# One trunk layer in fp32 on one core: where the newest pooling columns, the last channel sums and the first squares stand in their queues

## The chip, the core and the metric

The kernel runs on one core of a Trainium2 chip. The core has a matrix engine (TensorE; PE in the profile, its weight loads PEld), a vector engine (VectorE, DVE), an engine for functions and copies (ScalarE, ACT), a general engine (GpSimd, POOL) and a queue that mostly issues transfers (SyncE, SP). Each engine works through its own instructions in the order in which they were written into its queue; between engines they wait for each other by semaphores. The time of a run is the device time in microseconds (us) of one execution; less is better.

## The reference

One layer of a decoder trunk, for 256 columns of a new sequence and 8 x 4 newest tokens of running ones, together T = 288 columns:

```python
h = rmsnorm(x, norm1_g)
proj = h @ w_in + b_in                    # 2048 -> 3072
a, gate, z = proj[:1024], proj[1024:2048], proj[2048:]
u = a * sigmoid(gate)
c = silu(layernorm(depthwise_causal_conv(u_ext, conv_w, conv_b), ln_g, ln_b))   # 31 taps
d = multiscale_pool(z_ext)                # window means (2, 4, 8, 16) less z, 4 groups of 256 channels
p = (d @ pool_w, by group) * pool_scale
x = x + concat(c, p) @ w_out              # 2048 -> 2048
f = square(relu(rmsnorm(x, norm2_g) @ w_ff1))     # 2048 -> 8192
x = x + f @ w_ff2                         # 8192 -> 2048
y = rmsnorm(x, norm_f)
```

The last 30 columns of u and the last 15 of z are outputs as well. Everything is fp32.

## The kernel before

Channels lie on the 128 partitions, the 288 columns along the free axis. Each product of fp32 numbers is made of three products of rounded ones: a number is split into a high part (a rounded copy) and a low part (what is left), and TensorE adds up high x high, low x high and high x low. So each weight tile of 128 x 1024 numbers (a *part*, four blocks of 128 rows by 256 output channels) is loaded by SyncE, cast to its high part by ScalarE (L274, in `split_part`), and its low part is made in one of three *ways*: V, one subtraction on VectorE (L279); G, two subtractions of half a part on GpSimd (L282); D, a negated copy on ScalarE (L276) onto which GpSimd's queue adds the weights with an accumulating transfer (L277). `WAYS` (line 73) gives the way of each part by stage, in letters that repeat: stage "p" (the pooling groups without an entry of their own) has "GVVG". There are five buffers for split parts (line 101, `wspl`), and they are filled in the order in which TensorE uses them. The split of the next stage's weights is written down at the end of the present stage's `gemm`.

The input projection runs in the order of `SEQUENCE`: c0 c1 c2 c3 c4 p3 c5 p2 P3 c6 p1 P2 p0 P1 c7 P0. A *c* stage multiplies the columns of `a` and `gate` for 128 conv channels; a lower-case *p* stage the two blocks of z of one pooling group; a capital *P* is the small product of that group's differences with `pool_w`. A p or c stage is 16 blocks of rows by two banks by three products, four parts in all; each part is used over a quarter of the stage. The list `chain` sets TensorE's order to the order of writing up to P1. All else is ordered by a planner, which sorts instructions on each engine by a priority (the place in the program, moved by `later(...)`) and its own costs; `tc.issue_after(x)` puts an instruction behind x in the queue of x's engine.

`pool_group(g)` has these steps: the gemm; `tz`, bank times row factor, on VectorE (L483); z = tz + bias on ScalarE (L486, L487); the window sums by doubling, one add for each half and each doubling, on GpSimd (L492; group 1, window 4, has 4 adds, group 2 has 6, group 3 has 8); the first columns rescaled on GpSimd (L496); the difference for the sequence's columns on VectorE (L497); two steps on GpSimd for the newest columns (L499 scales, L500 subtracts), which overlap the same tile and stand behind L497; then the high copy (L502) and low part (L503).

`conv_pair(i)` scales its two banks by the row factor (L445), makes the gate's sigmoid (L447) and u (L449), and then, at a priority 1,000,000 later, 31 multiply-adds on VectorE for the sequence (L461) and one multiply on GpSimd (L464) with a reduction on VectorE (L466) for the newest columns. `sum_c` collects the channel sums for the layernorm's mean on GpSimd (L469 for pairs, L472 for the last ones).

At the start nine matmuls on constants (L214) run while inputs arrive. `first_split` casts and splits the first weights and the input; `squares` and `rsqrt_sums` make the first row factors from ScalarE's squares, TensorE's sums and a square root with a Newton step (L233 to L236 or the like); `spread` copies the factors to all partitions by three matmuls. In the layernorm `ln_mean`, `ln_sums` and `ln_rows` run between blocks of w_out's first gemms (`BETWEEN`), which start with the pooled half. At the end the last row sums give the factors of the final norm, and `finish` multiplies and stores the output in pieces.

Of the kernel before, what the change touches and what calls it, by code (L numbers as in the profile page):

```python
# [9 lines left out]
F32 = mybir.dt.float32  # L10
# [62 lines left out]
WAYS = {"c2": "GVGV", "c3": "GDGG", "c4": "GDGD", "p3": "GDDG", "c5": "GDGD", "c": "GGGV", "p": "GVVG", "w0": "VV", "w": "GG", "ff": "VV"}  # L73
# [13 lines left out]
def trunk_kernel(ctx: ExitStack, tc: tile.TileContext, io):  # L87
# [119 lines left out]
    def load_table(func, src):  # L207

        return nc.scalar.activation(few[: src.shape[0], :], src, func)

    load_table(AF.Sqrt, ones[:, 0:1])
    warm = ms("warm")
    for j in range(9):
        nc.tensor.matmul(warm[:, 0, 0:P], ones, ones, start=True, stop=True)  # L214
# [16 lines left out]
    def inverse_root(mean, root, y, out):  # L231

        nc.vector.reciprocal(y, root)  # L233
        nc.vector.scalar_tensor_tensor(out=root, in0=mean, scalar=EPS, in1=y, op0=ALU.add, op1=ALU.mult)
        nc.vector.scalar_tensor_tensor(out=root, in0=root, scalar=-0.5, in1=y, op0=ALU.mult, op1=ALU.mult)
        nc.vector.scalar_tensor_tensor(out=out, in0=root, scalar=1.5, in1=y, op0=ALU.add, op1=ALU.mult)  # L236

    def rsqrt_sums(parts, scale, after=None):

        pq = ms("pt")
        pt = pq[:, 0, :]
        for n, t in enumerate(parts):
            for j in range(3):
                last = mm(pt[:TB, j : j + 1], t[:, j * TB : (j + 1) * TB], ones[:, 0:1], start=n + j == 0, stop=n == len(parts) - 1 and j == 2)
        st = const.tile([TB, 12], F32, name=nm("st"))
        s = [st[:, 3 * j : 3 * j + 3] for j in range(4)]
        nc.vector.tensor_scalar(s[0], pt[:TB, 0:3], scale * DC, EPS, op0=ALU.mult, op1=ALU.add)
        nc.scalar.activation(s[1], s[0], AF.Sqrt)  # L250
        if after is not None:
            load_table(after, s[1][:, 0:1])
        nc.vector.reciprocal(s[2], s[1])
        nc.vector.tensor_tensor(s[3], s[2], s[2], op=ALU.mult)
        nc.vector.scalar_tensor_tensor(out=s[3], in0=s[3], scalar=-0.5, in1=s[0], op0=ALU.mult, op1=ALU.mult)
        nc.vector.scalar_tensor_tensor(out=s[2], in0=s[3], scalar=1.5, in1=s[2], op0=ALU.add, op1=ALU.mult)
        return s[2], pq[:, 1, :T], last
# [8 lines left out]
    turns = {}  # L266

    def split_part(raw, src, hi, lo, way):
# [6 lines left out]
        if way == "D":  # L275
            nc.scalar.activation(lo, f32(hi), AF.Copy, scale=-1.0)  # L276
            nc.gpsimd.dma_start(lo, src, accum_op=ALU.add)  # L277
        elif way == "V":
            nc.vector.tensor_tensor(lo, raw, f32(hi), op=ALU.subtract)  # L279
        else:  # L280
            for j in range(0, raw.shape[1], 2):
                nc.gpsimd.tensor_tensor(lo[:, j : j + 2, :], raw[:, j : j + 2, :], f32(hi[:, j : j + 2, :]), op=ALU.subtract)  # L282
# [74 lines left out]
    hx, firsts = [], []  # L357

    def first_split(k0):
# [5 lines left out]
        for k in range(k0, k0 + 2):  # L365
            if k == 0:
                nc.vector.tensor_scalar(hx[k][0], xT[:, k, :], v("norm1_g", k), None, op0=ALU.mult)  # L367
            else:
                nc.scalar.activation(hx[k][0], xT[:, k, :], AF.Copy, scale=v("norm1_g", k))  # L369
        for b in blocks[1:]:  # L370
            nc.scalar.copy(hi[:, b], raw[:, b])
        for b in blocks:
            nc.vector.tensor_tensor(lo[:, b], raw[:, b], f32(hi[:, b]), op=ALU.subtract)
# [37 lines left out]
    def squares():  # L411

        nc.scalar.copy(scratch[:, :, :, 0:1], f32(firsts[2][0])[:, 1, 1, 0:10].rearrange("p (n k t) -> p n k t", n=5, t=1))
        for q in range(8):
# [3 lines left out]
            nc.scalar.activation(dst, xq, AF.Square)  # L418
# [21 lines left out]
    def conv_pair(i, banks):  # L440
        up = u_all[:, i, 0:UO]
        us = samples(u_all[:, i, UO:UL], US)
        ta, gate = [b[:, :T] for b in banks]
        for b in (gate, ta):
            nc.vector.tensor_tensor(b, b, rb, op=ALU.mult)  # L445
        tg = tmpp.tile([P, 2, T], F32, name=nm("tg"), tag="ag", bufs=2)[:, 0, :]
        nc.scalar.activation(tg, gate, AF.Sigmoid, bias=v("b_in", 8 + i))  # L447
        for out, a, b in ((up[:, CH:UO], ta[:, :SEQ], tg[:, :SEQ]), (us[:, :, CH:US], samples(ta[:, SEQ:T], NS), samples(tg[:, SEQ:T], NS))):
            nc.vector.scalar_tensor_tensor(out=out, in0=a, scalar=v("b_in", i), in1=b, op0=ALU.add, op1=ALU.mult)  # L449
# [3 lines left out]
        with later():  # L453
# [10 lines left out]
            nc.gpsimd.tensor_tensor(prd[:, :, :, 0:CW], windows(us, CW), cwv[:, None, None, :].to_broadcast([P, NB, NS, CW]), op=ALU.mult)  # L464
# [12 lines left out]
    def pool_group(g):  # L477
# [17 lines left out]
        first_sums = s[:, :, PH : PH + w - 1]  # L495
        nc.gpsimd.tensor_tensor(first_sums, first_sums, rcnt[:, None, w - 2 : 2 * w - 3].to_broadcast([P, 2, w - 1]), op=ALU.mult)  # L496
        nc.vector.scalar_tensor_tensor(out=d[:, :, 0:SEQ], in0=s[:, :, PH:ZO], scalar=1.0 / w, in1=z[:, :, PH:ZO], op0=ALU.mult, op1=ALU.subtract)  # L497
        news = [x[:, :, ZO:ZL].rearrange("p m (b t) -> p m b t", t=ZS)[:, :, :, PH:] for x in (s, z)]
        nc.gpsimd.tensor_scalar(news[0], news[0], 1.0 / w, None, op0=ALU.mult)  # L499
        nc.gpsimd.tensor_tensor(d[:, :, SEQ:T].rearrange("p m (b t) -> p m b t", t=NS), news[0], news[1], op=ALU.subtract)  # L500
        dh, dl = act2("dx", tag="p", bufs=4)
        nc.scalar.copy(dh, d)  # L502
        nc.vector.tensor_tensor(dl, d, f32(dh), op=ALU.subtract)  # L503
        dd[g] = dh, dl

# [18 lines left out]
    def first_sums():  # L524
        diag.append(rsqrt_sums(squares(), 1.0 / D, AF.Sigmoid))
# [22 lines left out]
    load_table(AF.Sqrt, f32(mixp[1][0])[:, 0:1])  # L548
# [12 lines left out]
    def ln_sums():  # L561
        ssc = None
        for c in cs:
            nc.vector.tensor_tensor(c, c, norm["mean"][:, None, :].to_broadcast([P, 2, T]), op=ALU.subtract)
            q = tmpp.tile([P, 2, T], F32, name=nm("q2"), tag="ag" if ssc is None else "ag2", bufs=2)
            nc.scalar.activation(q, c, AF.Square)
            if ssc is None:
                ssc = q
            else:
                nc.vector.tensor_tensor(ssc, ssc, q, op=ALU.add)  # L570
        nc.vector.tensor_tensor(ssc[:, 0, :], ssc[:, 0, :], ssc[:, 1, :], op=ALU.add)
        norm["sums"] = rsqrt_sums([ssc[:, 0, :]], 1.0 / DC, AF.Silu)
        return norm["sums"][2]

    def ln_rows():
        norm["rows"], last = spread(norm["sums"])
        return last

    BETWEEN = {5: {4: ln_mean}, 6: {6: ln_sums}, 7: {2: ln_rows}}
# [10 lines left out]
    for j, c in enumerate(cs):  # L590
        n = tmpp.tile([P, 2, T], F32, name=nm("n"), tag="ag", bufs=2)
        nc.vector.tensor_tensor(n, c, norm["rows"][:, None, :].to_broadcast([P, 2, T]), op=ALU.mult)  # L592
        for m in range(2):
            i = 2 * j + m
            nc.scalar.activation(n[:, m, :], n[:, m, :], AF.Silu, bias=v("ln_b", i), scale=v("ln_g", i))  # L595
        mh, ml = act2("mx")
        nc.scalar.copy(mh, n)  # L597
# [40 lines left out]
    def second_rows():  # L638
# [9 lines left out]
        nc.scalar.activation(root, mean, AF.Sqrt, bias=eps)  # L648
        inverse_root(mean, root, r2, r2)
# [134 lines left out]
```

## Time and profile before

| what | value |
|---|---|
| median of 3 runs | 1084.99 us (1084.27 to 1086.06) |
| profiled execution | 1084.57 us, span 1082.8 us |
| TensorE busy | 1071.5 us in 8198 matmuls |
| VectorE, ScalarE, GpSimd busy | 635.4, 479.0, 173.6 us |
| HBM read, written | 185.16 MB, 4.28 MB |

The span is the time from the first to the last recorded instruction. Rows of a timeline begin with the start in us from the span's start and the duration; then come engine, line, operation, "out<-in" by the program's names, sizes, the count of merged instructions, and in brackets the idle time before and what ended it. A row of the waits says who waited for whom, how long in all, how often. The pooling stages and the conv lie in the first 200 us; w_out, w_ff1 and w_ff2 fill the rest.

### The profile page before, as it was taken

Reading aid. Unit: us, or ns where it says so; the run is one execution under the profiler, and the core shown is the slowest. Engines: PE = TensorE matmul, PEld = TensorE weight load, DVE = VectorE, ACT = ScalarE, POOL = GpSimd, SP = SyncE. Lnnn points to the kernel's source line nnn. Section 1 sums busy time; section 2 is a strip of 40 time slices with the busy share of each in tenths; the row PEclk is TensorE's granted clock in tenths of the full one; section 3 lists DMA queues with packets and bytes.
Section 4 is the critical chain, followed back from the end, with each engine's and each line's share of the span. In section 5 each row is a group of like instructions: output and inputs, shape, how many; then the busy total and the mean of one; then the engine's idle time right before and its main releaser. Section 6 shows DMA issues by size and latency. Waiting matters only on the chain.

```text
span 1082.8 us, 19572 instructions
## 1 busy us (share of the span) xinstructions
PE 1071.5 (99%) x8198; PEld 1069.9 (99%) x8198; DVE 635.4 (59%) x818; ACT 479.0 (44%) x585; POOL 173.6 (16%) x180
## 2 busy tenths in 40 slices
PE   9999999999999999999999999999999999999996
PEld 9999999999999999999999999999999999999996
DVE  8899999678655544445544444545544445554553
ACT  8654445475544433334443333444433334444441
POOL 0878979512000000000000000000000000000001
PEclk9999999999999999999999999999999999999998
DMA  9896468545555555555555555555555555555522
GB/s 325 281 273 185 137 196 239 176 152 177 173 164 170 172 166 169 174 164 169 171 168 168 175 165 169 174 167 167 174 165 168 174 169 165 173 166 168 173 78 88
DMA packets 58296, 190.71 MB, mean 176 GB/s; under 512 B 6240, under 2 KB 11232, under 8 KB 58208
## 3 DMA queue, kind: packets, MB, share of 16 engines
q1 hardware_dynamic: 56336, 184.35, 53.9%
q0 software_dynamic: 1008, 3.67, 1.9%
q8 instruction: 64, 1.05, 0.4%
q10 hardware_dynamic: 864, 1.44, 0.4%
q14 instruction: 24, 0.20, 0.1%
HBM read 185.16 MB, written 4.28 MB: 175 GB/s over the span
## 4 chain that ended last, share of the span: by engine, by line
PE 77%; issue 20%; ACT 1%; DVE 0%; DMA 0%; POOL 0%; POOLq 0%
PE ac L305 77%; PE pp L305 1%; DMA wr<-in_w 0%; ACT whi L274 0%; POOL xT L720 0%; ACT n L595 0%; DVE wlo L279 0%; PE pt L305 0%; PE pmean L305 0%; POOLq L770 0%; DVE xT L695 0%; DVE n L592 0%; ACT whi L364 0%; ACT mx L597 0%; DVE hx L367 0%
## 5 line engine op out<-in xcount | busy, mean ns | idle before, releaser
L274 ACT CAST whi<-wr 128x1024 fp32r<-128x1024 f32 (+1 forms) x332 | 348.0, 1049 | 551.4 <-PE ac L305 533.5
L279 DVE TENSOR_TENSOR wlo<-wr,whi 128x1024 fp32r<-128x1024 f32 x288 | 353.1, 1226 | 348.5 <-ACT whi L274 348.5
L305 PE MATMUL ac<-ax,whi 128*128 128x288 f32 x2048 | 351.0, 292 | 0.0
L305 PE MATMUL ac<-fx,whi 128*128 128x288 f32 x2048 | 350.2, 292 | 0.0
L305 PEld LDWEIGHTS ac<-ax,whi 128*128 128x128 f32 x2048 | 296.0, 187 | 0.0
L305 PEld LDWEIGHTS ac<-fx,whi 128*128 128x128 f32 x2048 | 295.6, 187 | 0.0
L305 PE MATMUL ac<-ax,wlo 128*128 128x288 f32 x1024 | 217.4, 292 | 0.0
L305 PE MATMUL ac<-fx,wlo 128*128 128x288 f32 x1024 | 216.4, 292 | 0.0
L305 PEld LDWEIGHTS ac<-ax,wlo 128*128 128x128 f32 x1024 | 162.6, 187 | 0.0
L305 PEld LDWEIGHTS ac<-fx,wlo 128*128 128x128 f32 x1024 | 162.3, 187 | 0.0
L305 PE MATMUL ac<-hx,whi 128*128 128x288 f32 x768 | 131.8, 295 | 1.2 <-DVE hx L367 1.2
L720 POOL TENSOR_TENSOR xT<-xT,rf 128x288 f32<-128x288 f32 x4 | 3.1, 795 | 800.1 <-ACT rf L724 800.1
L305 PEld LDWEIGHTS ac<-hx,whi 128*128 128x128 f32 x768 | 112.1, 190 | 1.4 <-ACT hx L369 1.4
L282 POOL TENSOR_TENSOR wlo<-wr,whi 128x512 fp32r<-128x512 f32 x74 | 100.3, 1410 | 35.3 <-ACT whi L274 34.3
L461 DVE SCALAR_TENSOR_TENSOR pc<-u_all,vec,pc 128x256 f32<-128x256 f32 x232 | 99.5, 483 | 1.9 <-ACT pc L458 0.7
L305 PE MATMUL ac<-hx,wlo 128*128 128x288 f32 x384 | 80.1, 294 | 0.0
L305 PEld LDWEIGHTS ac<-hx,wlo 128*128 128x128 f32 x384 | 61.1, 190 | 0.0
L305 PE MATMUL ac<-dx,whi 128*128 128x288 f32 x256 | 46.0, 296 | 0.0
L305 PE MATMUL ac<-mx,whi 128*128 128x288 f32 x256 | 45.1, 294 | 0.1
L664 DVE SCALAR_TENSOR_TENSOR t<-ac,r 128x576 f32<-128x576 f32 x32 | 24.2, 758 | 25.1 <-PE ac L305 25.1
L305 PEld LDWEIGHTS ac<-dx,whi 128*128 128x128 f32 x256 | 38.0, 188 | 0.2
L305 PEld LDWEIGHTS ac<-mx,whi 128*128 128x128 f32 x256 | 37.5, 188 | 0.6 <-ACT mx L597 0.4
(133 smaller groups left out, 533.6 us busy)
## 6 DMA issues: line engine op xcount, KB each, us to landing
wr<-in_w SPq DMA_DIRECT2D x335, 512.0 KB, 3.8
wlo<-in_w POOLq DMA_DIRECT2D x7, 512.0 KB, 7.7
xT<-in_xT SPq DMA_DIRECT2D x8, 288.0 KB, 7.3
wr<-in_w SPq DMA_DIRECT2D x5, 256.0 KB, 3.6
out_u_out<-u_all SPq DMA_DIRECT2D x1, 1208.0 KB, 9.3
u_all<-in_hist_c SPq DMA_DIRECT2D x8, 136.0 KB, 6.2
out_z_out<-z_all SPq DMA_DIRECT2D x1, 668.0 KB, 9.9
z_all<-in_hist_p SPq DMA_DIRECT2D x4, 152.0 KB, 7.5
```

Of the source, the lines that this page charges most:

```text
L274: nc.scalar.copy(hi, raw)
L279: nc.vector.tensor_tensor(lo, raw, f32(hi), op=ALU.subtract)
L282: nc.gpsimd.tensor_tensor(lo[:, j : j + 2, :], raw[:, j : j + 2, :], f32(hi[:, j : j + 2, :]), op=ALU.subtract)
L305: last = nc.tensor.matmul(*args, **kw)
L461: nc.vector.scalar_tensor_tensor(out=dst, in0=up[:, w : w + SEQ], scalar=cwv[:, w : w + 1], in1=pc, op0=ALU.mult, op1=ALU.add)
L664: nc.vector.scalar_tensor_tensor(out=t, in0=bk[:, :, :T], scalar=0.0, in1=both(rows2[0]), op0=ALU.max, op1=ALU.mult)
L720: eng.tensor_tensor(xk, xk, r[:, None, :].to_broadcast([P, n, T]), op=ALU.mult)
```

## The change

- `pool_group`: GpSimd's two steps on the newest columns (L499, L500) are written ahead of VectorE's difference (L497), so that the difference now stands behind them; for groups 1 and 0 all steps from L496 on have a priority 1,000,000 earlier. The difference is kept in `behind_pool`, and each low part of way V that is written afterwards is put behind it in VectorE's queue.
- `WAYS`: c2's fourth part becomes L, a subtraction on VectorE that is written later, behind the first bank scalings; c3's and c4's second parts go from D to V; c7 and p0 get their own entries, "GGGG" and "GVGG".
- `conv_pair`: the last two channel sums are written with the last channel block and put behind its multiply on GpSimd. The bank scalings of the first four banks move to `first_rows`.
- Start: 13 warm-up matmuls instead of 9; each square stands behind a high part of the input on ScalarE, the first low parts behind the first high part on VectorE.
- `inverse_root`: the reciprocal square root comes from one function of ScalarE, with the same Newton step; the reciprocal on VectorE is gone. All four norms use it, and the constants' placement changes with it.
- Layernorm: `ln_rows` two blocks earlier; the silus of the second to fourth pair stand behind the previous pair's copy on ScalarE.
- End: one output piece of two blocks is cut in two.

```diff
-WAYS = {"c2": "GVGV", "c3": "GDGG", "c4": "GDGD", "p3": "GDDG", "c5": "GDGD", "c": "GGGV", "p": "GVVG", "w0": "VV", "w": "GG", "ff": "VV"}
+WAYS = {"c2": "GVGL", "c3": "GVGG", "c4": "GVGD", "p3": "GDDG", "c5": "GDGD", "c7": "GGGG", "c": "GGGV", "p0": "GVGG", "p": "GVVG", "w0": "VV", "w": "GG", "ff": "VV"}
...
-    load_table(AF.Sqrt, ones[:, 0:1])
+    load_table(AF.Abs_reciprocal_sqrt, ones[:, 0:1])
     warm = ms("warm")
-    for j in range(9):
+    for j in range(13):
...
-    def inverse_root(mean, root, y, out):
-        nc.vector.reciprocal(y, root)
...
+    def inverse_root(mean, y, t, out, after=None):
+        nc.scalar.activation(y, mean, AF.Abs_reciprocal_sqrt, bias=eps[: y.shape[0], :])
+        if after is not None:
+            load_table(after, y[:, 0:1])
+        nc.vector.scalar_tensor_tensor(out=t, in0=mean, scalar=EPS, in1=y, op0=ALU.add, op1=ALU.mult)
...
         elif way == "V":
-            nc.vector.tensor_tensor(lo, raw, f32(hi), op=ALU.subtract)
+            with tc.issue_after(behind_pool[0]) if behind_pool else nullcontext():
+                nc.vector.tensor_tensor(lo, raw, f32(hi), op=ALU.subtract)
+        elif way == "L":
+            late.append((lo, raw, f32(hi)))
...
+            with tc.issue_after(scaled_x[min(q + 2, 7)]):
+                nc.scalar.activation(dst, xq, AF.Square)
...
-            if i == N8 - 2:
-                for part in (sum_c[:, 1, :], c):
-                    nc.gpsimd.tensor_tensor(sum_c[:, 0, :], sum_c[:, 0, :], part, op=ALU.add)
+            if i == N8 - 1:
+                for part in (sum_c[:, 1, :], cs[i // 2][:, 0, :]):
+                    with tc.issue_after(multiplied.ins):
+                        nc.gpsimd.tensor_tensor(sum_c[:, 0, :], sum_c[:, 0, :], part, op=ALU.add)
...
-        nc.vector.scalar_tensor_tensor(out=d[:, :, 0:SEQ], in0=s[:, :, PH:ZO], scalar=1.0 / w, in1=z[:, :, PH:ZO], op0=ALU.mult, op1=ALU.subtract)
...
+        with later(-LATER if g < 2 else 0):
...
+            nc.gpsimd.tensor_scalar(news[0], news[0], 1.0 / w, None, op0=ALU.mult)
+            nc.gpsimd.tensor_tensor(d[:, :, SEQ:T].rearrange("p m (b t) -> p m b t", t=NS), news[0], news[1], op=ALU.subtract)
+            pooled = nc.vector.scalar_tensor_tensor(out=d[:, :, 0:SEQ], in0=s[:, :, PH:ZO], scalar=1.0 / w, in1=z[:, :, PH:ZO], op0=ALU.mult, op1=ALU.subtract)
...
         dd[g] = dh, dl
+        behind_pool[:] = [pooled.ins]
...
     def first_rows():
-        pr, last = spread(diag[0])
-        nc.scalar.copy(rb, pr)
+        with later(-LATER):
+            pr, last = spread(diag[0])
+            nc.vector.tensor_copy(rb, pr)
+            for b in (pair0[1], pair0[0], pair1[1], pair1[0]):
+                scaled = nc.vector.tensor_tensor(b[:, :T], b[:, :T], rb, op=ALU.mult)
+        with tc.issue_after(scaled.ins):
+            nc.vector.tensor_tensor(*late.pop(), op=ALU.subtract)
...
-    BETWEEN = {5: {4: ln_mean}, 6: {6: ln_sums}, 7: {2: ln_rows}}
+    BETWEEN = {5: {4: ln_mean}, 6: {6: ln_sums}, 7: {0: ln_rows}}
...
+            with tc.issue_after(copied) if j else nullcontext():
+                nc.scalar.activation(n[:, m, :], n[:, m, :], AF.Silu, bias=v("ln_b", i), scale=v("ln_g", i))
...
-    finish(nc.vector, rows_f, ((0, 1), (1, 1), (2, 2), (4, 2), (6, 3), (9, 3)))
+    finish(nc.vector, rows_f, ((0, 1), (1, 1), (2, 1), (3, 1), (4, 2), (6, 3), (9, 3)))
```

More of the change, by code (lines that the diff above doesn't have):

```diff
@@ L264, in spread @@
         return pr, last
-    turns = {}
+    turns, late = {}, []
+    behind_pool = []
     def split_part(raw, src, hi, lo, way):
@@ L372, in first_split @@
         for b in blocks:
-            nc.vector.tensor_tensor(lo[:, b], raw[:, b], f32(hi[:, b]), op=ALU.subtract)
+            with tc.issue_after(first.ins) if k0 == 0 else nullcontext():
+                nc.vector.tensor_tensor(lo[:, b], raw[:, b], f32(hi[:, b]), op=ALU.subtract)
         for k in (k0 + 1, k0):
@@ L706, in trunk_kernel @@
                 nc.tensor.matmul(idle[:, 0:P], ones, ones, start=True, stop=True)
-    root, first, s_f = [cst[:TB, 2 + 3 * j : 5 + 3 * j] for j in range(3)]
-    nc.scalar.activation(root, sums_f, AF.Sqrt, bias=eps[:TB, :])
-    inverse_root(sums_f, root, first, s_f)
+    s_f = cst[:TB, 6:9]
+    inverse_root(sums_f, cst[:TB, 2:5], ends[:TB, 0, 4:7], s_f)
     for spread_f in (rows_f, again):
```

104 lines of the change are left out of this document (47 added, 57 removed).

## The prediction

> **What bounds the kernel now.** I read the busy shares first, then busy time by stretch, then the timelines of GpSimd, VectorE and TensorE around the pooling groups. The page and the table by stretch (columns: window, length, then busy time and count on TensorE, its weight loads, VectorE, ScalarE and GpSimd, granted clock, DMA share, GB/s) say:
>
> ```profile
> PE 1071.5 (99%) x8198; PEld 1069.9 (99%) x8198; DVE 635.4 (59%) x818; ACT 479.0 (44%) x585; POOL 173.6 (16%) x180
> ...
> L279 DVE TENSOR_TENSOR wlo<-wr,whi 128x1024 fp32r<-128x1024 f32 x288 | 353.1, 1226 | 348.5 <-ACT whi L274 348.5
> ```
> ```profile
> 6.40:10.40 4.00, 4.00 (x17) 4.00 (x18) 3.23 (x7) 3.17 (x7) 0.00 (x0) 1.00 1.05 407
> 10.40:14.00 3.60, 3.60 (x28) 3.60 (x28) 3.30 (x6) 3.56 (x8) 0.00 (x0) 1.00 1.05 409
> 300.00:400.00 100.00, 100.00 (x771) 100.00 (x770) 49.96 (x47) 41.31 (x44) 0.00 (x0) 1.00 0.54 169
> 1075.60:1078.00 2.40, 0.00 (x0) 0.00 (x0) 1.87 (x2) 0.00 (x0) 1.99 (x3) 0.50 0.99 375
> ```
>
> TensorE is busy 1071.5 us, and in the middle it never pauses: 771 matmuls in 100 us, 0.130 us each. So a gain elsewhere is worth nothing unless it removes a pause of TensorE, and few pauses are left: the start, the first slow matmuls, one hand-over in the layernorm, the tail. In contrast any new wait of TensorE is paid in full. That asymmetry decides this case. Faster or slower than no change can be told here from about 0.2% (2.2 us).
>
> **The change part by part.**
>
> *The low parts behind the pooling difference.* This is the part with a price. Each weight part (128x1024) is cut into a high part (ScalarE) and a low part; by way V VectorE makes the low part, 1.23 us each by the row of L279. The change sets each V part that is traced after a pooling group behind that group's difference (L497) in VectorE's queue, and puts GpSimd's L496, L499 and L500 ahead of the difference. TensorE takes parts in a fixed order, so what matters is when a V part is needed and when the difference ahead of it can run. By the order of tracing, p2's 2nd part comes behind group 3's difference, c6's 4th behind group 2's, p0's 2nd (its ways become GVGG) behind group 1's. The rows of need, on TensorE, with what VectorE does near them:
>
> ```profile
> 100.92 0.42 PE L305 MATMUL ac<-hx,wlo 128*128 128x288 f32 x2
> ...
> 121.20 0.42 PE L305 MATMUL ac<-hx,wlo 128*128 128x288 f32 x2
> ...
> 127.57 0.69 DVE L497 SCALAR_TENSOR_TENSOR d<-s,z_all 128x512 f32<-128x512 f32 x1 [0.96 <-POOL s L496]
> ...
> 137.65 0.74 DVE L483 TENSOR_TENSOR tz<-ac,rb 128x576 f32<-128x576 f32 x1
> ...
> 141.48 0.42 PE L305 MATMUL ac<-hx,wlo 128*128 128x288 f32 x2
> ```
>
> 100.92, 121.20 and 141.48 are the first uses of the low halves of those three parts. At 137.65 VectorE takes the sums of p1's gemm: only then do the columns of group 1 exist, 3.8 us before p0's 2nd part is needed. GpSimd from there on:
>
> ```profile
> 140.42 1.74 POOL L492 TENSOR_TENSOR s<-z_all 128x422 f32<-128x422 f32 x2
> 142.11 0.81 POOL L469 TENSOR_TENSOR sum_c<-sum_c,c 128x288 f32<-128x288 f32 x1
> 142.88 2.19 POOL L492 TENSOR_TENSOR s<-s 128x420 f32<-128x420 f32 x2
> 145.02 5.04 POOL L282 TENSOR_TENSOR wlo<-wr,whi 128x512 fp32r<-128x512 f32 x4
> 150.02 0.20 POOL L496 TENSOR_TENSOR s<-s,rcnt 128x6 f32<-128x6 f32 x1
> ```
>
> *p0.* The adds end at 140.42 + 1.74 + 0.81 + 2.19, about 145.1. The four low instructions at 145.02 are two parts of c7; p0's 2nd part now holds a buffer until TensorE has used it, which leaves room for one of them: 2.52, to 147.6. Then L496, L499 and L500 (0.20 here, 0.38 and 0.34 in the fence below) to 148.5, the difference 0.69 to 149.2, the low part 1.23 to 150.4. TensorE needs it at 141.48: **8.9 us of wait**. If GpSimd runs only group 1's steps (four adds at half of 1.74), they end at 143.9, the low part at 146.7, the wait is 5.2. With one more part ahead it is 8.9 + 2.52 = 11.4. I take 8.9: GpSimd's order in the row above, where a low part goes in ahead of L496; the ends are kept. Behind the waiting difference VectorE holds its low parts, the conv's multiply-adds and the next bank scalings; whoever waits for those is late by the same wait, as TensorE is, so I add nothing for it.
>
> ```profile
> 113.01 2.72 POOL L492 TENSOR_TENSOR s<-z_all 128x422 f32<-128x422 f32 x2
> 115.69 0.88 POOL L492 TENSOR_TENSOR s<-s 128x420 f32<-128x420 f32 x1
> 116.54 3.53 POOL L282 TENSOR_TENSOR wlo<-wr,whi 128x512 fp32r<-128x512 f32 x2
> 120.03 1.94 POOL L492 TENSOR_TENSOR s<-s 128x420 f32<-128x420 f32 x1
> 121.93 0.80 POOL L469 TENSOR_TENSOR sum_c<-c,c 128x288 f32<-128x288 f32 x1
> 122.70 1.71 POOL L492 TENSOR_TENSOR s<-s 128x416 f32<-128x416 f32 x2
> 124.37 2.98 POOL L282 TENSOR_TENSOR wlo<-wr,whi 128x512 fp32r<-128x512 f32 x2
> 127.31 0.22 POOL L496 TENSOR_TENSOR s<-s,rcnt 128x14 f32<-128x14 f32 x1
> 128.35 0.38 POOL L499 TENSOR_SCALAR s<-s 128x64 f32<-128x64 f32 x1 [0.81 <-DVE d L497]
> 128.81 0.34 POOL L500 TENSOR_TENSOR d<-s,z_all 128x64 f32<-128x64 f32 x1
> ```
>
> *c6.* The same pair of adds took 2.72 at 113.01 and 1.74 at 140.42, and other rows of this fence are long too; I read that as VectorE's low parts running beside them, and those now wait. So with the short durations: 113.01 + 1.74 + 0.88 + one low part 2.52 + 0.88 + 0.80 + 1.71 = 121.5; L496, L499, L500 0.94, to 122.5; difference 0.69, low part 1.23, to 124.4. Needed at 121.20: **3.2 us**. Lowest: six adds alone end at 118.2, and the part is ready at 121.1, no wait. Highest: another low part ahead, 5.7.
>
> ```profile
> 88.88 2.71 POOL L492 TENSOR_TENSOR s<-z_all 128x422 f32<-128x422 f32 x2
> 91.55 6.55 POOL L492 TENSOR_TENSOR s<-s 128x420 f32<-128x420 f32 x6
> 98.05 3.01 POOL L282 TENSOR_TENSOR wlo<-wr,whi 128x512 fp32r<-128x512 f32 x2
> 101.02 0.25 POOL L496 TENSOR_TENSOR s<-s,rcnt 128x30 f32<-128x30 f32 x1
> ```
>
> *p2.* The eight adds took 9.2 us and need 7.0 at 0.87 each; I take 7.6, to 96.5. The low part at 98.05 stays ahead of L496: 2.52, to 99.0; 0.25 + 0.38 + 0.34 to 100.0; difference and low part to 101.9, against 100.92: **1.0 us**. Ends: 0 when L496 goes first, 2.6 when the adds still end at 98.05.
>
> *The clock after a wait.* The first 17 matmuls of the gemm take 0.235 us (4.00 / 17), the next 28 take 0.129 (3.60 / 28). Getting back to speed thus costs 17 x 0.106 = 1.8 us. In the last row by stretch the granted clock is 0.50, with no matmul left. I charge 1.8 at the two long waits: **+3.6**, with 0 and 3.6 as ends. TensorE: Matmul & The Clock Gate, in the Trainium skill, says in Part 1 that the clock falls only after about one idle window of 3.4 us; by that rule the wait at c6 would keep it and the sum would be 1.8 lower. No row of this kernel shows TensorE idle for 3 us in its middle, so the trace can't settle it.
>
> *The start.* Warm-up matmuls go from 9 to 13:
>
> ```profile
> 1.04 4.21 PE L214 MATMUL warm<-ones 128*128 128x128 f32 x18 [1.04 <-DVE cst L229]
> 6.40 1.30 PE L305 MATMUL ac<-hx,whi 128*128 128x288 f32 x4 [1.15 <-DVE hx L367]
> ```
>
> 18 passes take 4.21, so 26 take 6.08 and end at 7.1: the first gemm starts 0.7 later, and without the break of 1.15. If the clock is up by then, 1.8 is saved: -1.1; a bit more where the ordered ScalarE and VectorE steps (high parts first, squares held back) bring data sooner. I take **-1.2**. Ends: +0.7 (slow as before) and -1.8. ScalarE is busy 3.56 of 3.60 from 10.40 on, so a faster TensorE may meet it there.
>
> *Inverse roots.* The function that gives 1/sqrt directly replaces a square root and L233. Four places; on TensorE's path are the first rows, the layernorm, the tail.
>
> ```profile
> 1071.57 0.17 DVE L233 RECIPROCAL cst<-cst 96x3 f32<-96x3 f32 x1 [1.53 <-ACT cst L708]
> ```
> ```profile
> 219.55 0.30 PEld L305 LDWEIGHTS ac<-mx,whi 128*128 128x128 f32 x2 [0.35 <-ACT mx L597]
> ```
>
> Tail: 0.17 and the hand-over after it, **-0.3** with the smaller output pieces (ends -0.6, +0.3). Layernorm: the rows are spread 12 matmuls sooner (12 x 0.130 = 1.6) and the silus queue behind the previous copy; TensorE waits 0.35 there for the first copy: **-0.5** (ends -0.8, +0.5, since the spread may wait itself). First rows: two VectorE steps fewer: **-0.1** (ends -0.3, +1.0). The number of table loads stays.
>
> *What I cost at nothing.* c3's and c4's 2nd parts go from ScalarE's negation with an accumulating DMA on GpSimd's queue to V: two DMA issues and two negations gone, 2 x 1.23 more on VectorE. c2's 4th waits for the bank scalings; c7's and p0's go to GpSimd, one low part each (2.52). Five part buffers let the splits run ahead of TensorE and hide these; without that cover each costs up to its own duration. The last channel sums (2 x 0.80) move behind c7's multiply on GpSimd; they are needed only in the sixth gemm of w_out, and cost 1.6 if late. Pooling's copies and low parts for groups 1 and 0 come sooner, to GEMMs that are then late anyway.
>
> *Sum.* 1084.57 (the profiled execution) - 1.2 - 0.1 - 0.5 - 0.3 + 8.9 + 3.2 + 1.0 + 3.6 = 1099.2. The median of the runs, 1084.99, stands 0.4 higher: **1099.5**.
>
> **The rivals.**
>
> *Only the shortest path (1).* GpSimd's pooling steps run ahead of the low parts and nothing stands between: 0 at p2 and c6, 5.2 at p0, one re-warming 1.8. 1084.99 - 2.1 + 5.2 + 1.8 = 1089.9. For it: the waits are known when the order is made, and group 1's steps are marked more urgent. Against it: the low parts at 98.05, 124.37 and 145.02 all stand ahead of L496.
>
> *More in front (2).* One low part more at c6 and at p0, 2 x 2.52, and VectorE's multiply-adds ahead of the difference, up to 1: 1105.5. For it: two low parts stand between group 2's adds, and two ahead of L496 at 145.02. Against: buffers.
>
> *The place in the queue costs nothing (3), the other side.* If the differences are done before the parts are needed, only the gains are left: 1084.99 - 2.1 = 1082.9. At p0 that decides: group 1's difference would have to start by 141.48 - 1.23 - 0.69 = 139.6, but its first add starts at 140.42. It holds only if the low part isn't in truth queued there.
>
> *Nothing to measure (4).* Waits near 2 in all meet the gains of 2.1: about 1085.
>
> **How the numbers follow.** Forecast 0.50, its own range 1094 to 1103 from the ends of p0 and of the clock; shortest path 0.27; more in front 0.13; queue costs nothing 0.07; nothing to measure 0.03. So slower 0.90, same 0.03, faster 0.07. From 1088 to 1106 hold the first three but for tails of about 0.07 of theirs, hence 0.83.
>
> **What the profile after would show.** A pause of TensorE of 5 to 9 us early in p0's gemm, released by VectorE's low part (L279's successor); ahead of it on VectorE group 1's difference, waiting for GpSimd; a smaller pause late in c6's gemm; some 17 matmuls at 0.235 us behind the long one. At the start the break of 1.15 gone, and fewer slow matmuls. GpSimd's two newest-column steps without a wait for VectorE. If no pause stands in p0's gemm, my reading of the queue is wrong; if it stands there and the time is still under 1088, one of the small gains is far larger than its row allows.

## The result, and the profile after

The changed kernel takes 1097.97 us in the median of 4 runs (1097.08 to 1098.60), the kernel before 1085.12 (4 runs): the ratio is 1.0118, with a 95% interval of 1.0100 to 1.0135. It is slower by 12.9 us, and 1099.5 had been forecast. The profiled execution of the changed kernel has a span of 1095.9 us, 13.1 more than before.

The page of the changed kernel: busy shares, the granted clock by slices, the chain that ended last, and the group of p's and c's low products.

```profile
PE 1075.9 (98%) x8206; PEld 1073.3 (98%) x8206; DVE 638.4 (58%) x814; ACT 474.8 (43%) x581; POOL 173.9 (16%) x182
...
PEclk9999989999999999999999999999999999999998
...
PE 70%; issue 20%; DVE 6%; DMA 1%; ACT 1%; POOL 0%; SPq 0%; POOLq 0%; DVEq 0%; ACTq 0%
...
L303 PE MATMUL ac<-hx,wlo 128*128 128x288 f32 x384 | 81.7, 298 | 3.7 <-DVE wlo L275 3.3
```

The same matmuls had no idle time ahead of them before; now 3.3 us of it end with VectorE's low parts (L275). VectorE stands in the chain with 6%. The sixth slice (137 to 164 us) is the only one in the middle with a lower clock. The waits of TensorE and its weight loads in the changed kernel (us in all, times, longest):

```profile
PEld pp L303 <- ACT dx L505: 4.7, 1, 4.7
PE pp L303 <- ACT dx L505: 4.5, 1, 4.5
...
PEld ac L303 <- DVE wlo L275: 4.1, 3, 2.3
...
PE ac L303 <- DVE wlo L275: 3.3, 3, 2.1
```

Both traces have 8118 matmuls over 288 columns on TensorE, so the n-th of one can be set against the n-th of the other. The difference of their starts (after less before) is worked out from those starts, and its steps are the ledger of the change:

| up to (time in before) | after less before, us | what stepped in between, us |
|---|---|---|
| 14.0 | -1.87 | start -1.87 |
| 36.0 | -1.38 | wait for the first sums +0.67, first rows -0.18 |
| 70.0 | -0.67 | wait for c4's last part +0.72 |
| 100.0 | -0.29 | evenly spread +0.38 |
| 102.0 | +0.59 | **p2's 2nd low part +0.88** |
| 120.0 | +1.04 | evenly spread +0.45 |
| 123.0 | +3.45 | **c6's 4th low part +2.41** |
| 140.0 | +3.88 | evenly spread +0.43 |
| 143.0 | +12.08 | **p0's 2nd part +8.20** |
| 150.0 | +13.62 | **slow matmuls after it +1.54** |
| 216.0 | +13.79 | +0.17 |
| 222.0 | +13.10 | layernorm -0.69 |
| 1060.0 | +13.09 | none |

The four bold rows make 13.0 us. The row of p0 holds 7.1 us of waiting, up to the first low product of p0's 2nd part; the other 1.1 are the first of the slow matmuls behind the wait, which take 0.24 us instead of 0.13. With 1.4 of the row below it the slow matmuls make 2.5; the last 0.1 of that row is the slower pace told next.

In the rows "evenly spread" TensorE doesn't wait. Its matmuls follow each other a little more slowly: from 104 to 119 us it has 115 of them in the changed kernel and 118 in the kernel before, at a granted clock of 1.00 in both. The first of these stretches begins right behind the wait for c4's last part, the second right behind p2's. The kernel without the queue edge (below) doesn't wait there and has 118. What makes the slower pace isn't shown.

Here is the largest of the bold rows: TensorE, then VectorE, then GpSimd in the changed kernel. L275 is the low part, L503 the difference, L499, L501 and L502 GpSimd's last pooling steps, L494 its adds. The row of 150.69 merges two low parts: p0's 2nd, of 128x1024, takes 2.28 us and ends at 152.98; the other is half as large.

```profile
144.87 0.69 PE L303 MATMUL ac<-hx,whi 128*128 128x288 f32 x4
146.57 0.53 PE L303 MATMUL ac<-hx,whi 128*128 128x288 f32 x2 [1.00 <-ACT whi L269]
151.58 0.85 PE L303 MATMUL pp<-dx,whi 128*128 128x288 f32 x2 [4.49 <-ACT dx L505]
153.03 0.85 PE L303 MATMUL ac<-hx,wlo 128*128 128x288 f32 x2 [0.60 <-DVE wlo L275]
153.68 1.16 PE L303 MATMUL ac<-hx,whi 128*128 128x288 f32 x4
```
```profile
148.78 1.26 DVE L462 SCALAR_TENSOR_TENSOR pc<-u_all,vec,pc 128x256 f32<-128x256 f32 x3
149.95 0.82 DVE L503 SCALAR_TENSOR_TENSOR d<-s,z_all 128x512 f32<-128x512 f32 x1
150.69 3.97 DVE L275 TENSOR_TENSOR wlo<-wr,whi 128x1024 fp32r<-128x1024 f32 x2
```
```profile
144.54 1.74 POOL L494 TENSOR_TENSOR s<-z_all 128x422 f32<-128x422 f32 x2 [2.13 <-ACT z_all L489]
146.23 1.74 POOL L494 TENSOR_TENSOR s<-s 128x420 f32<-128x420 f32 x2
148.04 0.20 POOL L499 TENSOR_TENSOR s<-s,rcnt 128x6 f32<-128x6 f32 x1
148.21 0.38 POOL L501 TENSOR_SCALAR s<-s 128x64 f32<-128x64 f32 x1
148.68 0.33 POOL L502 TENSOR_TENSOR d<-s,z_all 128x64 f32<-128x64 f32 x1
148.96 9.84 POOL L280 TENSOR_TENSOR wlo<-wr,whi 128x512 fp32r<-128x512 f32 x6
```

Between 145.6 and 153.0 us TensorE runs four matmuls: two high products at 146.57, two of the pooling product P1 at 151.58 (it now stands ahead of the low product), and only at 153.03 the first low product of p0's 2nd part. Ahead of that low part VectorE has group 1's difference, and ahead of that GpSimd's steps, as the prediction had it. Most of the pause is put down to ScalarE's high copy for P1 (4.49) and only 0.60 to the low part. But the low part ended at 152.98 and its first product began at 153.03, so TensorE would have waited as long for it without P1's two matmuls in between. The links differ in size, which the point by point part below takes up.

The other two places, on VectorE: p2's difference and low parts, and c6's.

```profile
97.45 0.47 DVE L446 TENSOR_TENSOR ac<-ac,rb 128x288 f32<-128x288 f32 x1 [0.85 <-PE ac L303]
97.83 0.87 DVE L462 SCALAR_TENSOR_TENSOR pc<-u_all,vec,pc 128x256 f32<-128x256 f32 x2
98.61 0.46 DVE L446 TENSOR_TENSOR ac<-ac,rb 128x288 f32<-128x288 f32 x1
98.97 1.23 DVE L503 SCALAR_TENSOR_TENSOR d<-s,z_all 128x512 f32<-128x512 f32 x1
```
```profile
121.01 1.23 DVE L503 SCALAR_TENSOR_TENSOR d<-s,z_all 128x512 f32<-128x512 f32 x1
122.17 4.51 DVE L275 TENSOR_TENSOR wlo<-wr,whi 128x1024 fp32r<-128x1024 f32 x2
```

### The profile page after: what moved, and what is told of

Read it like the earlier page. It is cut to its first block, busy times and chain, and to the rows that moved or that the text cites. A ratio compares the mean times of both kernels' runs of the same rounds, so it can differ in the third digit from the quotient of the medians.

```text
span 1095.9 us, 19586 instructions
## 1 busy us (share of the span) xinstructions
PE 1075.9 (98%) x8206; PEld 1073.3 (98%) x8206; DVE 638.4 (58%) x814; ACT 474.8 (43%) x581; POOL 173.9 (16%) x182
## 3 DMA queue, kind: packets, MB, share of 16 engines
q0 software_dynamic: 720, 2.62, 1.3%
q10 hardware_dynamic: 864, 1.29, 0.4%
## 4 chain that ended last, share of the span: by engine, by line
PE 70%; issue 20%; DVE 6%; DMA 1%; ACT 1%; POOL 0%; SPq 0%; POOLq 0%; DVEq 0%; ACTq 0%
PE ac L303 70%; DVE pc L462 3%; DVE wlo L275 1%; DMA wlo<-in_w 1%; DMA wr<-in_w 1%; DVE z_all L420 0%; DVE d L503 0%; DVE hx L376 0%; PE pp L303 0%; DVE wlo L373 0%; ACT hx L367 0%; ACT whi L362 0%; PE pt L303 0%; POOL xT L731 0%; DVE c L467 0%
## 5 line engine op out<-in xcount | busy, mean ns | idle before, releaser
L275 DVE TENSOR_TENSOR wlo<-wr,whi 128x1024 fp32r<-128x1024 f32 (+1 forms) x287 | 357.5, 1248 | 349.2 <-ACT whi L269 349.2
L280 POOL TENSOR_TENSOR wlo<-wr,whi 128x512 fp32r<-128x512 f32 x78 | 106.9, 1400 | 41.2 <-ACT whi L269 39.3
```

## The experiments

Ten kernels were run. The ratio is that of each to the kernel before on the same chip, with its 95% interval.

| kernel | median, us | before, us | ratio (interval) |
|---|---|---|---|
| after, no low part behind the difference | 1085.33 | 1084.76 | 1.0007 (0.9998 to 1.0016) |
| before, with that queue edge alone | 1092.79 | 1084.76 | 1.0079 (1.0065 to 1.0093) |
| after, p0's 2nd part alone without the edge | 1088.64 | 1084.76 | 1.0035 (1.0021 to 1.0049) |
| after, old order of difference and newest columns | 1094.73 | 1084.76 | 1.0089 (1.0073 to 1.0104) |
| after, edge on small products and w_out only | 1086.26 | 1084.89 | 1.0011 (1.0002 to 1.0020) |
| before, with the start alone | 1085.25 | 1084.89 | 1.0001 (0.9993 to 1.0010) |
| before, with start, inverse root, layernorm order | 1083.57 | 1084.89 | 0.9988 (0.9979 to 0.9997) |
| before, with eight delayed low parts | 1137.23 | 1084.89 | one run |
| after, no edge, old ways of p0 and c7 | 1087.93 | 1084.43 | 1.0027 (1.0016 to 1.0038) |
| after, no edge, no earlier pooling priority | 1085.81 | 1084.43 | 1.0015 (1.0004 to 1.0025) |

**Is it the place in VectorE's queue?** Theory: the low parts behind the difference make TensorE wait. Rival: the new order and priorities of the pooling steps do it.

```diff
         elif way == "V":
-            with tc.issue_after(behind_pool[0]) if behind_pool else nullcontext():
-                nc.vector.tensor_tensor(lo, raw, f32(hi), op=ALU.subtract)
+            nc.vector.tensor_tensor(lo, raw, f32(hi), op=ALU.subtract)
```

> The changed kernel, in which the low parts of way V are no longer put behind the pooling difference; all else as changed. Theory (the place in VectorE's queue costs the time): the waits at p2 (0.9), c6 (2.4) and p0 with the slow matmuls after it (10.0) go, some 13.3 us, so 1098.0 - 13.3 = 1084.7, between 1083.5 and 1086. Rival (the order of GpSimd's steps and the earlier priorities of the pooling steps cost it, or ScalarE's casts that come late): the waits in p0's gemm stay, the time stays above 1092.

Measured: 1085.33, within the theory's range, and the waits at p2, c6 and p0 are gone (the ledger stands at -1.20 from 36 to 156 us). Two other waits of TensorE came up, later than p0's: before P1's product, now for P1's low half, and at w_out's first low part. The waits of the weight loads in this kernel:

```profile
PEld ac L302 <- DVE wlo L274: 1.3, 1, 1.3
PEld pp L302 <- DVE dx L505: 1.1, 1, 1.1
```

So the edge costs about 12 us (1.18% less 0.07%), and without it the gains of the change (-1.2 and -0.7 in the ledger) are eaten by these two waits (+1.2 and +1.4 in the ledger).

The reverse, the edge alone in the kernel before (its difference L497 gets the name `pooled`):

```diff
         elif way == "V":
-            nc.vector.tensor_tensor(lo, raw, f32(hi), op=ALU.subtract)
+            with tc.issue_after(behind_pool[0]) if behind_pool else nullcontext():
+                nc.vector.tensor_tensor(lo, raw, f32(hi), op=ALU.subtract)
...
+        behind_pool[:] = [pooled.ins]
```

> The kernel before, with one thing of the change: the low parts of way V are put behind the pooling difference. Theory: the waits come, and longer ones than in the changed kernel, since GpSimd has a low part or two ahead of its last pooling steps there and WAYS is as before (p0's 2nd and 3rd part both by V): 13 to 20 us above the kernel before, 1098 to 1105. Rival (it takes the new GpSimd order or the priorities as well): within 2 us of the kernel before, 1083 to 1087.

Measured: 1092.79, 8.0 above the kernel before. The rival falls, and the theory's size was too high. The profiled execution is the slowest of the four, 1095.52 against 1092.75 to 1092.82 for the others, so its ledger ends 2.4 higher than the median shows, at +10.4. It has +0.04 at p2, +1.96 at c6, +6.93 at p0 and 0.40 after it. The waits of weight loads and matmuls in this kernel:

```profile
PEld ac L307 <- DVE wlo L281: 6.3, 2, 4.4
PE ac L307 <- DVE wlo L281: 5.9, 2, 4.2
```

Each of the two experiments (edge out of the new kernel, edge into the old) moves the time by most of the change. What the edge costs grows from 8 to about 12 us when the rest of the change is there.

**How much of it is p0?** Way U is way V without the edge; of the line of `WAYS` the entry that changes is shown.

```diff
...
-"p0": "GVGG"
+"p0": "GUGG"
...
+        elif way == "U":
+            nc.vector.tensor_tensor(lo, raw, f32(hi), op=ALU.subtract)
```

> The changed kernel, in which p0's 2nd part alone is not put behind the difference. Theory: the waits at p2 and c6 (3.3) stay, p0's (8.2) and the slow matmuls after it (1.5 to 1.9) go: 1088 to 1089. Rival (what is late at p0 is the whole chain, so the wait moves on to P1 or c7): above 1094.

Measured: 1088.64. Its ledger has p2 +0.90 and c6 +2.44 as in the changed kernel, and +0.07 where p0's +8.20 stood, with no slow matmuls. The wait didn't move on to P1 or c7. So the edge on this one low part of 128x1024 costs about 9 us (1.18% less 0.35%).

**What do GpSimd's two steps in front of the difference cost?** The line of `pooled` is put back above the two steps; the edge stays.

```diff
+            pooled = nc.vector.scalar_tensor_tensor(out=d[:, :, 0:SEQ], ...)
             news = [x[:, :, ZO:ZL].rearrange(...)[:, :, :, PH:] for x in (s, z)]
             nc.gpsimd.tensor_scalar(news[0], news[0], 1.0 / w, None, op0=ALU.mult)
             nc.gpsimd.tensor_tensor(d[:, :, SEQ:T].rearrange(...), news[0], news[1], op=ALU.subtract)
-            pooled = nc.vector.scalar_tensor_tensor(out=d[:, :, 0:SEQ], ...)
```

> The changed kernel with VectorE's difference ahead of GpSimd's two steps on the newest columns again, as before the change; low parts still behind the difference. Theory (these two steps are a small link of the chain, 0.38 + 0.34 and a hand-over at each of three places): about 1 us less at p0, 1 at c6, up to 1 at p2, so 1095 to 1097.5. Rival (GpSimd's two steps in front are what makes the difference late): most of the 13 us go, under 1090.

Measured: 1094.73, some 3 less, a little under the range of the theory and far from the rival's. In its ledger p2's step is +0.04 instead of +0.88, c6's +1.55 instead of +2.41, p0's with the slow matmuls 8.6 instead of 9.7. So GpSimd's two steps in front of the difference cost 0.8, 0.9 and 1.2 us at the three places, and only where the low parts stand behind the difference: the kernel without the edge has the same order and waits at none of them. In this kernel the edge costs about 9 us (0.89% less 0.07%), so most of what it costs beyond the 8 of the edge alone comes from this order.

**Can the edge be kept where it helps?** The two waits that came up without the edge suggested to keep it for the small pooling products and w_out's first block. The entries of `WAYS` that change:

```diff
...
-"c": "GGGV", "p0": "GVGG", "p": "GVVG"
+"c": "GGGU", "p0": "GUGG", "p": "GUUG"
```

> The changed kernel, in which only the low parts of the small pooling products and of w_out's first block still stand behind the difference; those of p2, c6, p1 and p0 do not. Theory: the waits at p2, c6 and p0 go, and the two new waits that appeared when the edge was taken away altogether (1.2 before P1, 1.4 at w_out's first low part) stay away, since the edge there keeps VectorE's multiply-adds and low parts in place: 1082.5 to 1084, 1 to 2 us under the kernel before. Rival (those two waits come from the other orders of the change, not from the edge): as without the edge, 1085 to 1086.

Measured: 1086.26, just above the rival's range and well above the theory's. Its ledger stands at -0.68 up to 150 us and rises by 2.48 to +1.80 at 160: 1.3 of it come where P1's products, which stand inside p0's gemm, wait for P1's low half. The kernel is not worth keeping.

**Where do these waits come from, then?** Two parts of the change were undone in the kernel without the edge: first the ways of p0 and c7 (entries of `WAYS`).

```diff
...
-"c7": "GGGG", "c": "GGGV", "p0": "GVGG", "p": "GVVG"
+"c": "GGGV", "p": "GVVG"
```

> The changed kernel without the edge, and with the ways of p0 and c7 as before the change (p0's 3rd and c7's 4th low part on VectorE instead of GpSimd). It asks where the two waits that appeared without the edge (1.2 before P1's product, 1.4 at w_out's first low part) come from. Theory (GpSimd's two extra low parts, 5.1 in all, push its last pooling steps back): both waits go, 2.5 less, 1082.8 to 1083.5. Rival (VectorE's queue, in which more low parts now stand ahead of the pooling low part): the waits stay or grow, 1085 to 1088.

Measured: 1087.93, over 2 us above the kernel that only lacks the edge. The theory falls: more low parts on GpSimd are not the cause. The step before P1 is about the same in the ledger (+1.06 instead of +1.21). The wait at w_out's first low part grew from 1.3 to 2.5, and 1.5 us of slow matmuls follow it:

```profile
PEld ac L302 <- DVE wlo L274: 2.5, 1, 2.5
```

That agrees with the rival, that more low parts stand ahead on VectorE's queue, but no run shows which instruction of VectorE is to blame. Then the priority of the pooling steps:

```diff
-        with later(-LATER if g < 2 else 0):
+        with later(0):
             first_sums = s[:, :, PH : PH + w - 1]
```

> The changed kernel without the edge, and without the earlier priority of the pooling steps of groups 1 and 0. Theory of the ways: nothing changes, 1085 to 1086. Rival (the earlier priority misplaces other work on VectorE and GpSimd): the two waits go, about 1083. If the priority protects P1: the wait before P1 grows from 1.2 to 3 or more, 1087 and up.

Measured: 1085.81 against 1085.33, with runs from 1084.98 to 1089.54 and overlapping intervals of the ratio: no difference that these runs can tell. What causes the two waits is left open. Its profiled execution is its slowest run and shows something else, told at the end.

**The start.** 13 warm-up matmuls and the first high part ahead of the low parts, in the kernel before:

```diff
-    for j in range(9):
+    for j in range(13):
...
-                nc.vector.tensor_scalar(hx[k][0], xT[:, k, :], ...)
+                first = nc.vector.tensor_scalar(hx[k][0], xT[:, k, :], ...)
...
+            with tc.issue_after(first.ins) if k0 == 0 else nullcontext():
                 nc.vector.tensor_tensor(lo[:, b], raw[:, b], f32(hi[:, b]), op=ALU.subtract)
```

> The kernel before with the start of the change alone: 13 warm-up matmuls, first low parts behind the first high part. Theory (the clock is up when the first gemm begins, so the slow matmuls of 0.240 us go): 0.8 to 1.9 us less than before, 1083 to 1084. Rival (the first gemm then waits for data as much as it gained, so the end does not move): within 0.4 us of before.

Measured: 1085.25, no gain (0.9993 to 1.0010). The rival holds. In its profiled execution 1.60 are won by 14 us and 0.90 given back between 14 and 36 us, most of it where TensorE, now at speed, meets a low part that stands behind the sums of squares on VectorE:

```profile
17.81 1.10 PEld L305 LDWEIGHTS ac<-hx,wlo 128*128 128x128 f32 x8 [0.47 <-DVE wlo L374]
17.81 1.34 PE L305 MATMUL ac<-hx,wlo 128*128 128x288 f32 x8 [0.24 <-DVE wlo L374]
```

The changed kernel's order of the squares keeps the 1.87 up to 28 us and pays 0.67 of it when the sums of the squares come late.

**The parts that gain, put together.** The start as above, the new `inverse_root` and `rsqrt_sums` with their calls, `ln_rows` two blocks earlier, the silus behind the previous copy, the layernorm's sums earlier in priority; all else as before.

```diff
+    def inverse_root(mean, y, t, out, after=None):
+        nc.scalar.activation(y, mean, AF.Abs_reciprocal_sqrt, bias=eps[: y.shape[0], :])
...
-    BETWEEN = {5: {4: ln_mean}, 6: {6: ln_sums}, 7: {2: ln_rows}}
+    BETWEEN = {5: {4: ln_mean}, 6: {6: ln_sums}, 7: {0: ln_rows}}
...
+            with tc.issue_after(copied) if j else nullcontext():
                 nc.scalar.activation(n[:, m, :], n[:, m, :], AF.Silu, ...)
```

> The kernel before with the start, the inverse root and the layernorm's order of the change, and nothing else of it: squares, first rows, pooling, conv, ways and output pieces as before. Theory: start -0.8 to -1.9, layernorm -0.7, tail -0.3, first rows about -0.2: 1081.7 to 1083. Rival (the gains of the changed kernel hang on its other orders): within 1 us of before.

Measured: 1083.57, 1.3 under the kernel before (interval 0.03% to 0.21%). It is the fastest of all kernels here, by less than expected, and a little beyond the rival's range too. Its profiled execution is its fastest run (1082.79); there the ledger has -0.65 after the first gemm, -0.20 at the first rows, -0.70 in the layernorm.

**When does the clock fall?** Eight low parts of the feed-forward stages are delayed by the same subtraction done again on half a part, 17 to 24 times; the result stays what it was.

```diff
+    MORE = {36: 17, 54: 18, 100: 19, 118: 20, 164: 21, 182: 22, 228: 23, 246: 24}
...
+            for _ in range(MORE.get(at[0], 0) if at[1] == "ff" else 0):
+                nc.vector.tensor_tensor(lo[:, 0:2, :], raw[:, 0:2, :], f32(hi[:, 0:2, :]), op=ALU.subtract)
             nc.vector.tensor_tensor(lo, raw, f32(hi), op=ALU.subtract)
```

> The kernel before, in which eight low parts of the second feed-forward product's weights (parts 36, 54, 100, 118, 164, 182, 228, 246) are preceded by 17 to 24 extra half subtractions into the same part, 0.6 to 0.7 us each, so that TensorE waits once for each, by lengths that grow in steps of about 0.65 us from about 1 to about 6. Theory of the prediction (the clock falls in any long wait): a wait from about 2 us on is followed by some 17 matmuls at 0.24. Rival (only a wait of about 3.4 us or more does it): waits up to about 3 us are followed by none, those above 4 by 10 to 20. Time: 1084.8 plus the waits, 1105 to 1130.

Measured: the waits didn't come as planned. At three of the places TensorE waited once, 1.1 us each, at four others four times in 9 us, the longest 2.7 us, at one not at all, and the run was longer than expected. After a wait of 1.1 us alone no slow matmul follows. After a wait of 2.7 us with one of 1.3 less than 2 us ahead, 19 and 21 matmuls at 0.24 us follow. After waits of 1.3 and 0.9 us with two matmuls in between, 14; after two of 1.3, 11. (These waits are taken from start to start of two matmuls, less the usual 0.13.) TensorE and the table by stretch around the two of 1.3 (window, length, busy time and count on TensorE, its loads, VectorE, ScalarE, GpSimd, granted clock, DMA share, GB/s):

```profile
340.37 0.53 PE L310 MATMUL ac<-ax,whi 128*128 128x288 f32 x2 [1.13 <-ACT whi L275]
342.08 0.85 PE L310 MATMUL ac<-ax,wlo 128*128 128x288 f32 x2 [1.18 <-DVE wlo L283]
342.72 1.16 PE L310 MATMUL ac<-ax,whi 128*128 128x288 f32 x4
```
```profile
338.90:342.50 3.60, 1.29 (x7) 0.82 (x6) 3.50 (x5) 1.04 (x1) 0.00 (x0) 0.90 0.05 15
342.50:345.10 2.60, 2.60 (x12) 2.60 (x12) 0.66 (x1) 0.00 (x0) 0.00 (x0) 0.50 0.63 184
345.10:350.00 4.90, 4.90 (x38) 4.90 (x38) 1.23 (x1) 1.18 (x2) 0.00 (x0) 0.99 0.32 117
```

Neither theory holds as it stood: it is not the length of one wait. In the 3.6 us before the fall TensorE was busy for 1.29. The wait at c6 in the changed kernel, 2.2 us by itself, left the clock alone:

```profile
121.00:124.50 3.50, 1.44 (x11) 1.21 (x10) 3.50 (x4) 1.62 (x2) 3.40 (x3) 1.00 0.00 0
124.50:130.00 5.50, 5.49 (x41) 5.49 (x42) 5.50 (x5) 0.62 (x1) 3.33 (x2) 1.00 0.76 267
```

That is 1.44 of 3.50, hardly more than 1.29 of 3.60, but these windows were cut by hand. The traces record when the granted clock changes, and in each trace the changes lie a whole number of 3.413 us apart: in the kernel of the eight delayed low parts it falls at 341.76 and is back at 345.17, one such stretch later, and falls again at 553.38, 62 after the first fall; in the changed kernel it falls at 147.97 and is back at 158.21, three later. So the stretches that count can be laid out from these times. TensorE's busy time in them (the ends of matmuls are modelled in the trace):

| kernel | stretch | TensorE busy, us | clock after it |
|---|---|---|---|
| eight delayed low parts | 338.34 to 341.76 | 1.43 | 0.50 |
| eight delayed low parts | 761.60 to 765.01 | 1.59 | 0.50 |
| after (p0) | 144.56 to 147.97 | 1.54 | 0.50 |
| before (tail) | 1072.11 to 1075.53 | 1.70 | 0.50 |
| after (c6) | 120.67 to 124.08 | 1.77 | 1.00 |
| after, p0's 2nd part alone without the edge (c6) | 120.55 to 123.97 | 1.87 | 1.00 |

In all twelve traces the clock fell behind each stretch that was busy for 1.70 or less, and behind none that was busy for 1.77 or more. So in these traces the busy time of a fixed stretch decides, not the length of one wait, with the limit near half of the stretch. The clock came back behind the first stretch that was busy for 3.04 or more; one of 2.62 left it at 0.50. TensorE: Matmul & The Clock Gate, in the Trainium skill, says in Part 1 that the clock falls after about one idle window of 3.4 us that runs freely. The length and the free running agree with these times; but the window need not be empty, it held up to 1.70 us of matmuls here.

## Why the prediction was right, point by point

**What bounds the kernel** was right: a wait of TensorE is paid in full, and every bold row of the ledger reaches the end.

**The queue edge** was right as the cause, by the first three experiments. Its three sizes:

- *p2*: forecast 1.0, measured 0.88. The way there was another. GpSimd's steps went ahead of its low part and were done at 97.16 by the prediction's own adds (7.4 us instead of 7.6); the difference then stood behind VectorE's bank scalings until 98.97 and took 1.23 instead of 0.69.
- *c6*: forecast 3.2, measured 2.41. No low part stood between GpSimd's adds, so that link was 2.5 shorter. In place of it the difference stood 0.6 behind VectorE's multiply-adds and took 1.23 instead of 0.69, and the two low parts at 122.17 took 4.51 together, 2.3 each instead of 1.23.
- *p0*: forecast 8.9, measured 7.1 (the 8.20 of the ledger less 1.1 of slow matmuls). "GpSimd's order in the row above, where a low part goes in ahead of L496" is the step that failed: GpSimd ran adds and last steps in one go from 144.54 to 149.01, 4.5 us instead of 8.1. What filled part of the place was VectorE's queue. The difference waited 0.9 behind multiply-adds, and the low part took 2.28 instead of 1.23. By the ledger the first add, at 140.42 before, should have come at 140.42 + 3.9 = 144.3; it came 0.2 later. So one link was 3.6 too long and the others some 2 too short: that the size came out near is in part luck.

**The clock** was charged twice, 3.6; it was paid once, 2.5 at p0 (1.1 within p0's row and 1.4 of the 1.54 below it): 20 matmuls at 0.24 us follow the wait, where some 17 were foretold. With it p0 cost 9.7, and 10.7 had been forecast. The step "I charge 1.8 at the two long waits" failed at c6. The page of the Trainium skill that the prediction set beside it, with a sum 1.8 lower, was right on that place: the clock stayed at 1.00 there.

**The gains** (2.1 forecast): start and first rows -1.2 and -0.1 against -1.87 and +0.49, so -1.3 against -1.38; layernorm -0.5 against -0.69; tail -0.3 against none (the last matmul came 0.27 sooner by the ledger, and the end of the span is no sooner; in the kernel of the parts put together, with six output pieces instead of seven, 0.26 stay). As a sum right; but the start alone is worth nothing in the runs. And the trace of one execution says little of it: the six other kernels with this start gain 0.79 to 1.66 by 14 us, where this one gained 1.87.

**What I costed at nothing** was not all nothing: c4's last part, by an accumulating DMA, came 0.72 late in this one profile, when TensorE was 1.4 earlier there. The six other kernels with the same way don't show it, at smaller leads. And 1.4 us come from the slower pace of the matmuls behind the waits, which the prediction doesn't have.

**The rivals.** The shortest path had the order on GpSimd right (nothing stood between) and missed VectorE's part of the chain; its 1089.9 was too low. The other side (the queue place costs nothing, 1082.9) falls: the place costs about 12 us. Nor does the kernel without the edge show the gains that it counted on: it takes 1085.33.

In all: 1084.57 - 1.38 + 0.72 + 1.43 + 0.88 + 2.41 + 8.20 + 1.54 - 0.69 = 1097.7, and the profiled execution took 1097.68. The forecast's terms add up to 14.6 (from 1084.99 that is 1099.6, where 1099.5 was written) and these to 13.1. Of the 13.1 the slower pace and c4's part, for which nothing was charged, make 1.43 and 0.72, so the waits and the clock alone were forecast 16.7 and came to 13.0. That the total is only 1.5 off is in part luck.

## What to carry to other kernels

Where one engine sets the end, an order put on another engine's queue is priced by what the ordered work waits for, not by its own length: a low part of 1.2 us that was put behind a difference cost about 9 us, since that difference hung on the engine that was to use the low part. So read for each instruction behind a new edge when it is needed and when the thing ahead of it can run at the earliest; here the first was 3.8 us after the gemm that the second needs. A gain at the start of a kernel should be followed to the next wait before it is counted.

## What the runs showed of the hardware that was not expected

In one execution a single VectorE instruction lasted about as long as GpSimd had work back to back. In the profiled execution of the kernel without the edge and without the earlier priority, the difference, 0.69 us in the kernel before, took 5.08. VectorE and GpSimd there:

```profile
154.59 0.48 DVE L461 SCALAR_TENSOR_TENSOR pc<-u_all,vec,pc 128x256 f32<-128x256 f32 x1
154.97 5.08 DVE L502 SCALAR_TENSOR_TENSOR d<-s,z_all 128x512 f32<-128x512 f32 x1
159.98 1.26 DVE L461 SCALAR_TENSOR_TENSOR pc<-u_all,vec,pc 128x256 f32<-128x256 f32 x3
```
```profile
155.00 0.32 POOL L501 TENSOR_TENSOR d<-s,z_all 128x64 f32<-128x64 f32 x1
155.28 2.52 POOL L279 TENSOR_TENSOR wlo<-wr,whi 128x512 fp32r<-128x512 f32 x2
157.78 1.73 POOL L493 TENSOR_TENSOR s<-z_all 128x422 f32<-128x422 f32 x2
159.58 0.53 POOL L498 TENSOR_TENSOR s<-s,rcnt 128x2 f32<-128x2 f32 x1
```

GpSimd runs five instructions from 155.00 to 159.5 without a gap; VectorE's difference ends only after that. TensorE waited 3.4 us for its result. SBUF — State Buffer, in the Trainium skill, says under SBUF: two separate sides that the two engines share a pair of ports, which one of them holds for a whole instruction. The rows agree in kind, and show more: VectorE's difference lasted across several instructions of GpSimd. That is no rule: in the changed kernel GpSimd ran six low halves back to back from 148.96 to 158.80, and the difference beside them, at 149.95, took 0.82. What sets the two cases apart isn't shown. Milder cases beside GpSimd's low halves are in the changed kernel (0.69 to 1.23 for the difference, 1.23 to 2.3 for a low part), and they are a part of what p0, c6 and p2 waited. Whether this also makes the spread of the runs of the kernel above, 1084.98 to 1089.54, was not shown.
